# Gated DeltaNet mixer: triangular inverses kept at 64x64 blocks, the rest solved on v with two heads on the partitions

## The chip, the cores and the metric

The kernel runs on one core of a Trainium2 chip. The metric is the device time of one execution in microseconds. Its engines are PE (TensorE, matrix products), DVE (VectorE), ACT (ScalarE), POOL (GpSimd) and SP (SyncE); the last two issue most of the DMAs here. They run side by side, each through its own list of instructions in order, and wait for one another on semaphores.

## The reference, cut to what matters

The program is a trunk of two layers over 256 tokens of width 2048, in f32. Layer 0 mixes tokens with a gated delta rule, layer 1 with sparse attention; behind each mixer stand a convolutional gated feed-forward block and a gated embedding. Only layer 0's mixer changes:

```python
proj = x @ w_in                                  # q, k, v, z and the gates
qkv = silu(causal_dwconv(qkv, conv_w))
diff = gc[..., :, None] - gc[..., None, :]
decay = where(tri, exp(where(tri, diff, 0.0)), 0.0)
lmat = where(strict, einsum('bhncd,bhnsd->bhncs', kb, k) * decay, 0.0)
amat = lmat + eye(C)
sol = triangular_solve(amat, rhs, left_side=True, lower=True, unit_diagonal=True)
```

`amat` is unit lower triangular, one for each head and chunk; solving with it on the values gives u, from which the outputs follow. The kernel works the same recurrence with chunks of 128 tokens, so that there are two blocks, `a = 0, 1`, a head. There are 32 value heads of width 128.

## The kernel before

**Plan.** The order of all instructions is written by a planner, `Plan`. Each piece of work is a task, made by `add(engine, cost, emit, after, ...)`, with an estimated cost, tasks it follows (`after` in data, `behind` in order only), buffers that it takes and gives back (`take`, `give`, counted in `room`), a `rank` (lower first) and, for DMAs, a `tail` until the data has landed. `run` simulates the engines with these costs and emits each task when its engine is free and its inputs and buffers are. The order of each engine is thereby fixed when the program is built; the chip only adds the waits. The big weight products form one strict sequence on PE (ranks 4 and 5); the mixer's small products have rank 1 and are put between them as soon as the planner sees them ready.

**Weights.** Weights come as blocks of 128 x 1024 f32 through SP into `raw`; ACT or DVE rounds them to `hi` (L412, L416), DVE forms `lo = raw - hi` (L420), and PE multiplies in fp32r (L349, L352; L362, L363, L365). Products of plain f32 show as two records each.

**Mixer.** Heads go in 8 groups of four (`g`, `i` within a batch), groups in two batches of four. `decay_gates` computes the cumulated gates and stores them in DRAM as `grow` (L734); `decays` brings them back as rows, broadcast over the partitions (L829, on SP), into L and qd. `batch` makes L = `lmat` for each group (L989, L995; gram products L869), stores its 32x32 diagonal blocks (`lt`, L1006, on POOL) and its lower blocks (`lo`, L1013), loads all the diagonal blocks of a batch with one block on each partition (`ld`, L1019), inverts them by substitution in 31 steps on DVE (L1037, L1039), and stores the inverses plain and transposed (`tt`, L1042; `tu`, L1045).

`solve` builds from these the 128x128 inverse of each head and block `a`. On the partitions lie four heads with 32 rows each. `Lb`, `Gc` and `Tb` are loaded by 8 DMAs each (L899, L908, L905). For block distance d = 2, 1, 0 it computes `left` (L924: 1, 2 and 3 products for each `a`, of 32 to 96 columns), an eviction on ACT (L928), `right` (L933: one product for each `a`) and another eviction (L936). `Gc` then goes to DRAM as `gs` (L944), and `group` loads it into `pm` by 8 DMAs (`fill`, L1119), where each head's inverse lies as one 128x128 matrix.

`group` transposes v (`turn`, L1103), scales it (L1108) and for each block `a` multiplies by `pm` (`begin`, L1086, by way of the helper `mul`; four products of 128 columns) and evicts to u (`keep`, L1150). Between the two blocks stand `cross` (also L1086, with `n21`) and `cut` (L1138). `out` (L1164, L1165), the norm and the transposes that fill `oT` follow. The output products of group g (`mixes`) are placed between the weight blocks of group g + 2; those of the last two groups come after the mixer, and `project` takes oT of groups 6 and 7. The planner's order around the change depends on: 2 PSUM buffers `bk` and 2 `sp`, one `vt`, one `pm`, one `u`, four `L`. `conv` makes q, k and v (L559 to L573).

## Time and profile before

| what | us |
|---|---|
| median of 3 runs | 2768.59 (2767.57 to 2770.47) |
| the profiled execution's own time | 2768.83 |
| its span, first to last instruction | 2767.0 |
| PE busy | 2749.2 |
| DVE busy | 1871.4 |
| ACT busy | 1441.1 |
| POOL busy | 251.3 |

The engines overlap, so their busy times don't add up to the span. The granted PE clock is 0.998 of full speed over the span. A row of a timeline has the start and length in us, engine, line, operation, written tile and read tiles, shapes and count, and in brackets the idle time before it and what ended it. A row of groups has a count, busy us and mean ns, then the idle time before. Matmuls are pipelined: their recorded lengths overlap, and the distance from start to start is what one costs.

### The profile page before, as it was taken

Reading aid. Unit: us, or ns where it says so; the run is one execution under the profiler, and the core shown is the slowest. Engines: PE = TensorE matmul, PEld = TensorE weight load, DVE = VectorE, ACT = ScalarE, POOL = GpSimd, SP = SyncE. Lnnn points to the kernel's source line nnn. Section 1 sums busy time; section 2 is a strip of 40 time slices with the busy share of each in tenths; the row PEclk is TensorE's granted clock in tenths of the full one; section 3 lists DMA queues with packets and bytes.
Section 4 is the critical chain, followed back from the end, with each engine's and each line's share of the span. In section 5 each row is a group of like instructions: output and inputs, shape, how many; then the busy total and the mean of one; then the engine's idle time right before and its main releaser. Section 6 shows DMA issues by size and latency. Waiting matters only on the chain.

```text
span 2767.0 us, 39746 instructions
## 1 busy us (share of the span) xinstructions
PE 2749.2 (99%) x14796; PEld 2373.6 (86%) x14796; DVE 1871.4 (68%) x2964; ACT 1441.1 (52%) x2314; POOL 251.3 (9%) x437
## 2 busy tenths in 40 slices
PE   9999999999999999999999999999999999999999
PEld 8878888888888888888888888988888888888887
DVE  7887679866778666666546766775766666655575
ACT  6766565655555455555434444455555555543343
POOL 0324212034000000000000000300000000000000
PEclk9999999999999999999999999999999999999999
DMA  7776657666655766665557456545656666655655
GB/s 216 221 216 179 183 172 218 191 177 194 173 164 184 220 192 209 209 198 186 195 191 238 158 185 216 173 153 169 194 173 195 199 195 192 196 192 190 214 173 190
DMA packets 418434, 531.43 MB, mean 192 GB/s; under 512 B 24476, under 2 KB 305792, under 8 KB 418240
## 3 DMA queue, kind: packets, MB, share of 16 engines
q1 hardware_dynamic: 401424, 499.81, 57.7%
q0 software_dynamic: 16128, 28.49, 3.8%
q8 instruction: 116, 1.90, 0.3%
q14 instruction: 78, 0.64, 0.1%
q10 hardware_dynamic: 688, 0.59, 0.1%
HBM read 517.74 MB, written 14.20 MB: 192 GB/s over the span
## 4 chain that ended last, share of the span: by engine, by line
PE 96%; DMA 2%; DVE 1%; POOL 0%; ACT 0%; issue 0%; SPq 0%; ACTq 0%
PE mm_ps L352 33%; PE mm_ps L349 17%; PE b_ps L362 13%; PE b_ps L363 13%; PE b_ps L365 13%; DMA raw<-in_gdn_w_in 1%; PE s_ps L1086 1%; PE s_ps L924 1%; PE o_ps L1165 1%; DMA pm<-gs 0%; PE n_ps L1397 0%; PE lg_ps L1736 0%; PE sc_ps L1653 0%; PE s_ps L933 0%; DMA tu<-ld 0%; DMA gs<-Gc 0%
## 5 line engine op out<-in xcount | busy, mean ns | idle before, releaser
L420 DVE TENSOR_TENSOR lo<-raw,hi 128x1024 fp32r<-128x1024 f32 (+1 forms) x906 | 1103.6, 1219 | 707.7 <-ACT hi L412 695.1
L412 ACT ACTIVATE hi<-raw 128x1024 fp32r<-128x1024 f32 (+1 forms) x871 | 918.3, 1054 | 1085.7 <-PE mm_ps L352 504.3
L352 PE MATMUL mm_ps<-xT,hi 128*128 128x512 f32 (+1 forms) x4136 | 1012.4, 393 | 3.8 <-DVE pd L562 2.6
L352 PEld LDWEIGHTS mm_ps<-xT,hi 128*128 128x128 f32 (+1 forms) x4136 | 755.8, 188 | 151.5 <-issue 3.7
L349 PEld LDWEIGHTS mm_ps<-xT,lo 128*128 128x128 f32 (+1 forms) x4136 | 532.2, 191 | 20.2
L349 PE MATMUL mm_ps<-xT,lo 128*128 128x256 f32 (+1 forms) x4136 | 544.3, 284 | 0.0
L362 PE MATMUL b_ps<-hi,xT 128*128 128x512 f32 (+2 forms) x678 | 260.4, 385 | 2.9 <-ACT hi L412 2.9
L363 PE MATMUL b_ps<-hi,xT 128*128 128x512 f32 (+2 forms) x678 | 258.3, 382 | 0.0
L362 PE MATMUL b_ps<-hi,hTA 128*128 128x512 f32 x512 | 199.2, 389 | 0.0
L363 PE MATMUL b_ps<-hi,hTA 128*128 128x512 f32 x512 | 199.2, 389 | 0.0
L365 PE MATMUL b_ps<-lo,xT 128*128 128x512 f32 (+2 forms) x678 | 180.7, 383 | 0.0
L362 PEld LDWEIGHTS b_ps<-hi,xT 128*128 128x128 f32 x678 | 127.8, 188 | 26.4 <-ACT hi L412 3.1
L363 PEld LDWEIGHTS b_ps<-hi,xT 128*128 128x128 f32 x678 | 127.9, 189 | 23.3
L365 PEld LDWEIGHTS b_ps<-lo,xT 128*128 128x128 f32 x678 | 124.8, 189 | 22.8
L365 PE MATMUL b_ps<-lo,hTA 128*128 128x512 f32 x512 | 136.9, 389 | 0.0
L1436 POOL DMA_DIRECT2D lng<-in_ln_g x16 | 8.7, 546 | 1335.8 <-DVE x L1442 1333.2
L363 PEld LDWEIGHTS b_ps<-hi,hTA 128*128 128x128 f32 x512 | 96.1, 188 | 20.0
L362 PEld LDWEIGHTS b_ps<-hi,hTA 128*128 128x128 f32 x512 | 96.1, 188 | 20.0
L365 PEld LDWEIGHTS b_ps<-lo,hTA 128*128 128x128 f32 x512 | 96.1, 188 | 19.9
L362 PE MATMUL b_ps<-hi,oT 128*128 128x512 f32 (+1 forms) x258 | 102.9, 399 | 0.1
L363 PE MATMUL b_ps<-hi,oT 128*128 128x512 f32 (+1 forms) x258 | 100.4, 389 | 0.0
L569 DVE SCALAR_TENSOR_TENSOR ac<-pd,cw,ac 128x256 f32<-128x256 f32 x192 | 90.6, 482 | 4.3 <-ACT ac L566 0.7
(333 smaller groups left out, 2599.6 us busy)
## 6 DMA issues: line engine op xcount, KB each, us to landing
raw<-in_gdn_w_in SPq DMA_DIRECT2D x191, 512.0 KB, 4.1
raw<-in_ffn_w_down SPq DMA_DIRECT2D x160, 512.0 KB, 3.9
raw<-in_ffn_w_up SPq DMA_DIRECT2D x158, 512.0 KB, 3.8
raw<-in_ffn_w_gate SPq DMA_DIRECT2D x157, 512.0 KB, 4.2
raw<-in_dsa_w_in SPq DMA_DIRECT2D x72, 512.0 KB, 3.6
raw<-in_gdn_w_o SPq DMA_DIRECT2D x64, 512.0 KB, 3.9
raw<-in_ple_w_gate SPq DMA_DIRECT2D x56, 512.0 KB, 4.4
raw<-in_dsa_w_o SPq DMA_DIRECT2D x32, 512.0 KB, 4.3
```

Source lines behind the costliest of these rows:

```text
L349: nc.tensor.matmul(ps[o][:m, S:], lo[:, k, o * P:o * P + m], xk[:, 0], start=False, stop=e)
L352: nc.tensor.matmul(ps[o][:m], hi[:, k, o * P:o * P + m], xk.rearrange("p a b -> p (a b)"), start=s, stop=e)
L362: nc.tensor.matmul(ps[o][:, c], xh, hi[:, k, c], start=s, stop=False)
L363: nc.tensor.matmul(ps[o][:, c], xl, hi[:, k, c], start=False, stop=False)
L365: nc.tensor.matmul(ps[o][:, c], xh, lo[:, k, c], start=False, stop=e and c.stop == n)
L412: nc.scalar.activation(hi, box["raw"], AF.Copy)
L420: nc.vector.tensor_tensor(lo, box["raw"], box["hi"].bitcast(F32), op=ALU.subtract)
L569: nc.vector.scalar_tensor_tensor(box["ac"], pd[:, k:k + S], wt[:, k:k + 1], box["ac"], op0=ALU.mult, op1=ALU.add)
L924: nc.tensor.matmul(ps[:, a, 32 * (e - d - 1):], Lb[:, a, PAIR[e, d]], Gc[:, a, e, 32 * e:], start=e == d + 1, stop=e == 3)
L1086: nc.tensor.matmul(ps[:, h], lhs[:, h], rhs[:, h], start=True, stop=True)
L1165: nc.tensor.matmul(ps[:, h], qd()[:, a, h], u()[:, a, h], start=not a, stop=True)
L1436: d = add(G, 0.55, lambda r=r, src=src: nc.gpsimd.dma_start(out=r(), in_=bass.AP(tensor=src.tensor, offset=src.offset + nb * 512, ap=[[0, ...
```

## The change

Inverses are built only up to 64x64. `solve` now has one level: `left` and `right` make four products each of 32 columns, one for each (block `a`, half `n`), with four heads on the partitions; two evictions go to `Gy` and `Gx`. `Lb`, `Gc` and `Tb` are loaded by 4 DMAs each. There is no `gs`: `group` fills the diagonal 32x32 blocks of `pm` straight from `tt` by 8 DMAs, and the off-diagonal block from `Gx` by 4 (`place_`, from SBUF to SBUF). A matrix in `pm` now holds two heads, each with a 64x64 inverse on its part of the diagonal.

The step from 64 to 128 is done on v: the upper half is multiplied by its inverse (`begin`, n = 0), copied to `ua`, multiplied by the lower left 64x64 block of L (`lower`), taken from the lower half of v (`minus`), which then meets its own inverse (`begin`, n = 1). That block of L is transposed on DVE (`flip`), stored in DRAM (`spare`, 4 DMAs a group) and loaded into `LB` (`across`, 4 DMAs). The right sides hold two heads on the partitions, 64 tokens each: the Silu of v's conv writes block 0 in that order (two calls, not one), and block 1 is brought to it by `less`, eight calls on 64 partitions that replace the four of `cut` and write to `vp`. The results are evicted to u by calls on 64 partitions that write to other partitions than they read (`keep`).

Beside that: `grow` is stored by two DMAs so that a group's rows are one run; the layout of L and qd is by head and then block; the `lo` stores are 2 a group, not 3; the scale `svp` is copied in that layout; some `tail`s given to the planner are larger; `vp`, `ua`, `LT`, `LB` and `Gx` are single buffers. The core of the diff:

```diff
-        pm, Tb, Lb, Gc = new("pm", [8, P]), new("Tb", [2, 3, P]), new("Lb", [2, 6, P]), new("Gc", [2, 4, P])
-        PAIR = {(e, d): e * (e - 1) // 2 + d for e in range(1, 4) for d in range(e)}
+        pm, Tb, Lb, LB = new("pm", [2, 4, P]), new("Tb", [4, P]), new("Lb", [4, P]), new("LB", [2, 2, P])
+        Gc, Gy, Gx = (new(k, [4, 32]) for k in ("Gc", "Gy", "Gx"))
...
+                        nc.scalar.activation(tile()[:, 0].rearrange("p (n r t) -> p n r t", n=2, r=2)[:, :, c],
+                                             box["ac"][:, :P].rearrange("p (n t) -> p n t", n=2), AF.Silu)
+                        nc.scalar.activation(tile()[:, 1, c * P:c * P + P], box["ac"][:, P:], AF.Silu)
...
-                self.grow = self.dr.tile([64, P], F32, tag="grow", name="grow", bufs=1)
-                nc.gpsimd.dma_start(out=self.grow, in_=gr)
+                self.grow = self.dr.tile([32, 2, P], F32, tag="grow", name="grow", bufs=1)
+                for a in range(2):
+                    nc.gpsimd.dma_start(out=self.grow[:, a], in_=gr[32 * a:32 * a + 32])
...
         def rows_into(g, dm):
-            nc.sync.dma_start(out=dm, in_=bass.AP(tensor=self.grow.tensor, offset=self.grow.offset + 4 * g * P,
-                                                  ap=[[0, P], [32 * P, 2], [1, 4 * P]]))
+            nc.sync.dma_start(out=dm.rearrange("p h a t -> p (h a t)"),
+                              in_=bass.AP(tensor=self.grow.tensor, offset=self.grow.offset + 8 * g * P,
+                                          ap=[[0, P], [1, 8 * P]]))
...
         def solve(s, i):
 
...
+            def spread(tile, name, first):
+                def put(h):
+                    hs = slice(32 * h, 32 * h + 32)
+                    src = s[name][i, h].rearrange("a b p c -> p (a b) c")[:, first::2]
+                    nc.gpsimd.dma_start(out=tile[hs, :, hs] if tile is not Gc else tile[hs], in_=src)
+                return put
...
+            tt, tu = [], []
+            for tile, name, key, first, got, rank in ((Gc, "tt", "t", 1, tt, R["fetch"]), (Tb, "tu", "u", 0, tu, R["fetch"])):
+                put = spread(tile, name, first)
+                for h in h4:
+                    got.append(add(G, 0.55, lambda h=h, put=put: put(h), [s[key]], behind=got[-1:],
+                                   take=["Gc" if tile is Gc else "Tb"] * (not h), tail=5.0, rank=rank))
+            s["lb", i] = []
+            for n in h4:
+                s["lb", i].append(add(G, 0.55, lambda n=n: across(n), s["LT", i],
+                                      behind=s["lb", i][-1:] or s.get(("lb", i - 1), chained["lb"])[-1:],
+                                      take=["LB"] * (not n), tail=4.0, rank=R["keep"]))
+            chained["lb"] = s["lb", i]
...
+            def left():
+                ps = box["ps"] = sps("bk", [4, 32], "s_ps")
+                for n in h4:
+                    nc.tensor.matmul(ps[:, n], Lb[:, n], Gc[:, n], start=True, stop=True)
+
+            def right():
+                ps = box["ps"] = sps("bk", [4, 32], "s_ps")
+                for n in h4:
+                    nc.tensor.matmul(ps[:, n], Tb[:, n], Gy[:, n], start=True, stop=True)
+            y = add(E, 0.9, left, [*lo, *tt], take=["bk", "Gx"], give=["Lb", "Gc"], rank=1)
+            y = add(A, 0.3, lambda: nc.scalar.activation(Gy, box["ps"], AF.Copy), [y], give=["bk"], rank=1)
+            y = add(E, 0.9, right, [y, *tu], take=["bk"], give=["Tb"], rank=1)
+            s["x", i] = add(A, 0.3, lambda: nc.scalar.activation(Gx, box["ps"], AF.Identity, scale=-1.0), [y],
+                            give=["bk"], rank=1)
+
+        chained = dict(lb=[], pm=[])
...
+                        nc.gpsimd.dma_start(out=s["lt"][i, :, :, c].rearrange("h a i j -> i (h a) j"),
+                                            in_=ha(L[g]()[32 * c:32 * c + 32, :, :, 32 * c:32 * c + 32]))
+                    stored.append(add(G, 0.6, store, [p], tail=3.5))
+                LT = lazy(lambda: new("LT", [8, 64]))
+
+                def flip(g=g, LT=LT):
+                    nc.vector.transpose(LT()[64:], ha(L[g]()[64:, :, :, :64]))
+                f = add(V, 0.6, flip, [p], take=["LT"], rank=3)
+                s["LT", i] = []
+                for n in range(4):
+                    def spare(n=n, i=i, LT=LT):
+                        e, d = n // 2, n % 2
+                        nc.gpsimd.dma_start(
+                            out=s["lb"][i, :, :, 32 * d:32 * d + 32, 32 * e:32 * e + 32].rearrange("h a p c -> p (h a) c"),
+                            in_=LT()[64 + 32 * e:96 + 32 * e, :, 32 * d:32 * d + 32])
+                    s["LT", i].append(add(G, 0.6, spare, [f], give=["LT"] * (n == 3), behind=s["LT", i][-1:], tail=4.0,
+                                          rank=R["keep"]))
...
-                    def keep(e=e, g=g, i=i):
+                for n in range(2):
+                    def keep(n=n, g=g, i=i):
                         nc.gpsimd.dma_start(
-                            out=s["lo"][i, :, :, PAIR[e, 0]:PAIR[e, 0] + e].rearrange("q i d j -> i q (d j)"),
-                            in_=L[g]()[32 * e:32 * e + 32, :, :, :32 * e].rearrange("p a h j -> p (a h) j"))
-                    s[i].append(add(G, 0.6, keep, [p], give=["L"] * (e == 3), tail=3.0, rank=R["keep"]))
...
                 def turn(j=j, box=box):
                     ps = box["ps"] = sps("sp", [2, 2, P], "v_ps")
-                    for a in range(2):
-                        for r in range(2):
-                            nc.tensor.transpose(ps[:, a, r], VT[g][j]()[:, r, a * P:(a + 1) * P], self.ident)
+                    for n in range(2):
+                        nc.tensor.transpose(ps[:, 0, n], VT[g][j]()[:, 0, n * P:n * P + P], self.ident)
+                    for r in range(2):
...
-                for a in range(2):
-                    def fill(a=a, d=d):
-                        nc.gpsimd.dma_start(out=pm[32 * d:32 * d + 32, 4 * a:4 * a + 4, 32 * d:],
-                                            in_=s["g", i][:, :, a, d, 32 * d:].rearrange("h j c -> j h c"))
-                    ld.append(add(G, 0.55, fill, [s["st", i]], behind=ld[-1:], take=["pm"] * (not ld), tail=3.0, rank=R["fill"]))
+            for h in h4:
+                j, r = h // 2, h % 2
+                for e in range(2):
+                    def fill(h=h, j=j, o=64 * r + 32 * e, e=e):
+                        nc.gpsimd.dma_start(out=pm[o:o + 32, j, :, o:o + 32],
+                                            in_=s["tt"][i, h].rearrange("a b p c -> p (a b) c")[:, e::2])
+                    ld.append(add(G, 0.55, fill, [s["t"]] if ld else [s["t"], s["x", i]], behind=ld[-1:] or chained["pm"], take=["pm"] * (not ld), tail=5.0,
+                                  rank=R["fill"]))
+            for h in h4:
+                def place_(h=h, j=h // 2, o=64 * (h % 2)):
+                    nc.gpsimd.dma_start(out=pm[o:o + 32, j, :, o + 32:o + 64], in_=Gx[32 * h:32 * h + 32])
+                ld.append(add(G, 0.55, place_, [s["x", i]], behind=ld[-1:], give=["Gx"] * (h == 3), tail=4.0, rank=R["fill"]))
+            chained["pm"] = ld[-1:]
 
             qd, qo, n21, wq, fd, wd = fr[g]
             v_ = R["last"] if last else 2
             u, ud = lazy(lambda: new("u", [2, 4, P])), []
+            vp = lazy(lambda: new("vp", [4, P]))
...
+                    def less(n, j, box=box):
+                        ns = slice(64 * n, 64 * n + 64)
+                        for r in range(2):
+                            h = 2 * j + r
+                            nc.vector.scalar_tensor_tensor(
+                                vp()[64 * r:64 * r + 64, 2 * j + n], box["ps"][ns, h], s["nc1"][ns, 4 * i + h:4 * i + h + 1],
+                                vt()[ns, 1, h], op0=ALU.mult, op1=ALU.add)
+                    x = add(E, 0.95, cross, [*d, fd[1]], take=["bk"], give=["n21"], rank=1)
+                    d = []
+                    for n in range(2):
+                        for j in range(2):
+                            x = add(V, 0.5, lambda n=n, j=j, less=less: less(n, j), [x, *td], take=["vp"] * (not n and not j),
+                                    give=["bk", "L" if last else "vt"] if n and j else [], rank=v_)
+                        d.append([x])
+                else:
+                    d = [d, d]
+                last_of = []
...
+                    box = {}
+
+                    def begin(a=a, n=n, y=y, box=box):
+                        ps = box["ps"] = sps("bk", [2, P], "s_ps")
+                        for j in range(2):
+                            nc.tensor.matmul(ps[:, j], pm[:, j, 2 * a + n], y()[:, 2 * j + n], start=True, stop=True)
+
+                    def keep(r, a=a, n=n, box=box):
+                        return (u()[64 * n:64 * n + 64, a].rearrange("p (j r) c -> p r j c", r=2)[:, r],
+                                box["ps"][64 * r:64 * r + 64])
+                    x = add(E, 0.45, begin, [*d[n], *(ld if not n and not a else [])], take=["bk"],
+                            give=["pm", "vp"] if a and n else [], rank=1)
+                    if not n:
+                        ua = lazy(lambda: new("ua", [2, P]))
+                        z = add(A, 0.41, lambda ua=ua, box=box: nc.scalar.activation(ua(), box["ps"], AF.Copy), [x],
+                                take=["ua"], rank=0.8)
+                        more = {}
+
+                        def lower(a=a, ua=ua, more=more):
+                            ps = more["ps"] = sps("sp", [2, P], "s_ps")
+                            for j in range(2):
+                                nc.tensor.matmul(ps[:, j], LB[:, j, a], ua()[:, j], start=True, stop=True)
+
+                        def minus(y=y, more=more):
+                            t = y().rearrange("p (j n) c -> p n j c", n=2)[:, 1]
+                            nc.vector.tensor_tensor(t, t, more["ps"], op=ALU.subtract)
+                        z = add(E, 0.45, lower, [z, *s["lb", i]], take=["sp"], give=["ua"] + ["LB"] * a, rank=1)
+                        z = add(V, 0.42, minus, [z, *d[1]], give=["sp"], rank=min(v_, 1.5))
+                        d[1] = [z]
+                    for r in range(2):
+                        last_of.append(add(A, 0.41, lambda r=r, keep=keep: nc.scalar.activation(*keep(r), AF.Copy), [x],
+                                           take=["u"] * (not a and not n and not r), give=["bk"] * r,
+                                           behind=last_of[-1:] + ([z] if not n else []) if 0 else last_of[-1:], rank=1))
+                d = last_of
+                ud.append(last_of)
```

More of the change, by code (lines that the diff above doesn't have):

```diff
@@ L264, in build @@
         nc.gpsimd.memset(Lb, 0.0)
[L265 removed]
+        nc.gpsimd.memset(LB, 0.0)
         box1 = {}
@@ L747, in decay_gates @@
             y = add(V, 0.8, six, [y], give=["sp"], rank=1)
-            rows["go"] = add(G, 0.6, store, [y, b], tail=2.0)
+            rows["go"] = add(G, 1.2, store, [y, b], tail=2.0)
         rows = {}
@@ L892, in solve @@
         def solve(s, i):
-            wait, back = [], []
-            for q in range(8):
-                a, hs = q // 4, slice(32 * (q % 4), 32 * (q % 4) + 32)
-                def left(q=q, a=a, hs=hs):
-                    nc.gpsimd.dma_start(out=Lb[hs, a, :, hs], in_=s["lo"][i, q])
-                back.append(add(G, 0.55, left, s[i] if not q else [], behind=back[-1:], take=["Lb"] * (not q), tail=3.0, rank=R["keep"]))
-            def fetch(q, what):
-                a, hs = q // 4, slice(32 * (q % 4), 32 * (q % 4) + 32)
-                if what:
-                    nc.gpsimd.dma_start(out=Tb[hs, a, :, hs], in_=s["tu"][i, q, :3].rearrange("b n c -> n b c"))
-                    return
-                base = Gc[hs, a]
-                nc.gpsimd.dma_start(out=bass.AP(tensor=base.tensor, offset=base.offset,
-                                                ap=[list(base.ap[0]), [P + 32, 4], [1, 32]]),
-                                    in_=s["tt"][i, q].rearrange("b c n -> c b n"))
@@ L911, in solve @@
-            for what in range(2):
-                for q in range(8):
-                    back.append(add(G, 0.55, lambda q=q, what=what: fetch(q, what), [s["u"] if what else s["t"]],
-                                    behind=back[-1:], take=["Tb" if what else "Gc"] * (not q), tail=3.0, rank=R["fetch"]))
-            y = back
-            for d in (2, 1, 0):
-                n = 32 * (3 - d)
-                box = {}
-                def left(d=d, n=n, box=box):
-                    ps = box["ps"] = sps("bk", [2, n], "s_ps")
-                    for a in range(2):
-                        for e in range(d + 1, 4):
-                            nc.tensor.matmul(ps[:, a, 32 * (e - d - 1):], Lb[:, a, PAIR[e, d]], Gc[:, a, e, 32 * e:],
-                                             start=e == d + 1, stop=e == 3)
-                def keep(n=n, box=box):
-                    nc.scalar.activation(Gc[:, :, 3, :n], box["ps"], AF.Copy)
-                def right(d=d, n=n, box=box):
-                    ps = box["ps"] = sps("bk", [2, n], "s_ps")
-                    for a in range(2):
-                        nc.tensor.matmul(ps[:, a], Tb[:, a, d], Gc[:, a, 3, :n], start=True, stop=True)
-                def less(d=d, box=box):
-                    nc.scalar.activation(Gc[:, :, d, 32 * (d + 1):], box["ps"], AF.Identity, scale=-1.0)
-                y = add(E, 0.41 * (3 - d) + 0.05, left, y if d == 2 else [y], take=["bk"], give=["Lb"] * (not d), rank=1)
-                y = add(A, 0.2 + 0.0018 * n, keep, [y], give=["bk"], rank=1)
-                y = add(E, 0.46, right, [y], take=["bk"], give=["Tb"] * (not d), rank=1)
-                y = add(A, 0.2 + 0.0018 * n, less, [y], give=["bk"], rank=1)
@@ new lines, in across @@
+            def across(n):
+                j, r = n // 2, n % 2
+                rs = slice(64 * r, 64 * r + 64)
+                nc.gpsimd.dma_start(out=LB[rs, j, :, rs], in_=s["lb"][i, n].rearrange("a p c -> p a c"))
+            lo = []
+            for h in h4:
+                lo.append(add(G, 0.55, lambda h=h: nc.gpsimd.dma_start(
+                    out=Lb[32 * h:32 * h + 32, :, 32 * h:32 * h + 32],
+                    in_=s["lo"][i, h].rearrange("a b p c -> p (a b) c")),
+                    s[i], behind=lo[-1:], take=["Lb"] * (not h), tail=4.0, rank=R["keep"]))
@@ L1009, in batch @@
-                    stored.append(add(G, 0.6, store, [p], tail=2.5))
+                        nc.gpsimd.dma_start(out=s["lt"][i, :, :, c].rearrange("h a i j -> i (h a) j"),
[4 more added lines that the diff above has]
+                    nc.vector.transpose(LT()[64:], ha(L[g]()[64:, :, :, :64]))
@@ L1171, in sq @@
                                              accum_out=ss()[:, a, h // 2, h % 2:h % 2 + 1])
-                x = add(E, 1.85 if a else 0.95, out, [ud[a if last else 1], *fd], take=["bk"], give=["u", "qo", "qd"] if a else [], rank=1)
+                x = add(E, 1.85 if a else 0.95, out, [*ud[a if last else 1], *fd], take=["bk"], give=["u", "qo", "qd"] if a else [], rank=1)
                 for hs in ((0, 1), (2, 3)):
```

105 lines of the change are left out of this document (46 added, 59 removed).

## The prediction

> **What bounds the kernel now.** I read the page's engine totals and the chain of waits first, then busy time by stretch, then PE's waits.
>
> ```profile
> span 2767.0 us, 39746 instructions
> ...
> PE 2749.2 (99%) x14796; PEld 2373.6 (86%) x14796; DVE 1871.4 (68%) x2964; ACT 1441.1 (52%) x2314; POOL 251.3 (9%) x437
> ...
> PE 96%; DMA 2%; DVE 1%; POOL 0%; ACT 0%; issue 0%; SPq 0%; ACTq 0%
> ```
>
> PE (TensorE) is busy for all but 17.8 us, and 96% of the chain that ended last is PE's own work. So a change counts in two ways only: by PE time taken out or put in, and by moments at which PE stands still. The change touches the first mixer, which fills about the first 820 us. Each row below gives the stretch, its length, and busy us (instructions) of PE, then (second fence) of PE, PE's weight loads, DVE, ACT and POOL.
>
> ```profile
> 0.00:300.00 300.00, 287.92 (x1624) 0.99 0.70 204
> 300.00:800.00 500.00, 499.66 (x2789) 1.00 0.64 186
> ```
> ```profile
> 100.00:200.00 100.00, 94.44 (x491) 80.77 (x490) 85.50 (x167) 61.23 (x112) 26.76 (x48) 0.98 0.73 218
> ...
> 400.00:500.00 100.00, 99.84 (x533) 85.89 (x532) 88.79 (x174) 58.78 (x120) 22.52 (x39) 1.00 0.67 196
> ```
>
> From 300 to 800 us PE is never idle (0.3 us); whatever is saved there on PE is saved in the end. In the first 300 us it stands still for 12.1 us, for these reasons among others (total, times, longest):
>
> ```profile
> PE b_ps L362 <- ACT hi L412: 2.9, 1, 2.9
> PE mm_ps L352 <- DVE pd L562: 2.6, 1, 2.6
> PE s_ps L1086 <- DMA pm<-gs: 1.5, 2, 0.8
> ...
> PE s_ps L933 <- DMA Tb<-tu: 1.2, 1, 1.2
> PE s_ps L924 <- DMA Tb<-tu: 1.1, 1, 1.1
> ```
>
> The last three, 3.8 us, belong to the inverses that the change rewrites.
>
> **PE work.** A matmul of plain f32 shows as two records. Per group of four heads, the code before makes 12 products in `left` (L924) and 6 in `right` (L933). The records bear it out: 192 = 8 groups x 12 x 2, 96 = 8 x 6 x 2.
>
> ```profile
> L924 PE MATMUL s_ps<-Gc,Lb x192: 190/275/329, 186.6 to 692.1; 128*128 128x32 f32 x96, 128*128 128x64 f32 x64, 128*128 128x96 f32 x32
> ```
> ```profile
> L933 PE MATMUL s_ps<-Gc,Tb x96: 190/275/276, 190.1 to 694.5; 128*128 128x32 f32 x32, 128*128 128x64 f32 x32, 128*128 128x96 f32 x32
> ```
>
> After it, `left` and `right` make 4 each, of 32 columns. The two products with `pm` stay at 4 each but are cut into halves of 2, and `lower` is new: 2 products of 128 columns for each of the two token blocks. So 18 + 8 = 26 products become 8 + 8 + 4 = 20, six fewer. The blocks in which they are sent stay at eight (six and two before; two, four and two after). What is one worth? The recorded 275 ns overlap, so I take start to start of whole blocks, from PE's timeline:
>
> ```profile
> 642.97 0.53 PE L924 MATMUL s_ps<-Gc,Lb 128*128 128x32 f32 x4
> 643.33 0.48 PE L362 MATMUL b_ps<-hi,xT 128*128 128x512 f32 x1
> ...
> 652.59 1.42 PE L924 MATMUL s_ps<-Gc,Lb 128*128 128x96 f32 x12
> 653.84 0.63 PE L1103 MATMUL v_ps<-ident,v 128*128 128x128 f32 x4
> ...
> 657.54 1.05 PE L1086 MATMUL s_ps<-vt,pm 128*128 128x128 f32 x8
> 658.35 2.10 PE L352 MATMUL mm_ps<-xT,hi 128*128 128x512 f32 x8
> ```
>
> Two products take 0.36 us, four 0.81, six 1.25: (1.25 - 0.36) / 4 = 0.2225 us for each further product, and a block's fixed part is the same before and after. The three have mostly 32, 128 and 32 to 96 columns and lie on one line, so the columns do not show. Six fewer are 1.34 us a group, **10.7 us** in eight groups. Bounds: 0.18 us a product (0.36 / 2) gives 8.6; nothing in the rows gives more than 0.2225. I take 10.7, as block counts are equal.
>
> The Trainium skill, TensorE: Matmul & The Clock Gate, section Back-to-back issue gap, speaks against this: there a warm matmul costs its columns / 2.4 GHz + 2.5 ns, by which the narrow products taken out would be nearly free and the 128-wide ones put in would not, and the net gain an estimated 1.9 us. The same page's section on LDWEIGHTS gives columns of the weights / 1.2 ns, some 107 ns a record whatever the moving width, an estimate of 0.21 us a product, and with that the rows agree.
>
> **Waits of the solve.** Of the 3.8 us, the 1.5 on `pm<-gs` lose their cause: the trip of `Gc` to DRAM and back (`gs`) is gone, `pm`'s diagonal comes straight from `tt`. The 2.3 on `Tb<-tu` stay possible: `right` still waits for `Tb`, though for 4 loads, not 8. Bounds 0 to 3.8 saved; I take the middle, 1.9, since the chain as a whole gets shorter:
>
> ```profile
> 167.33 0.55 POOL L1042 DMA_DIRECT2D tt<-xi  x1 [45.92 <-DVE wq L822]
> 171.31 0.54 POOL L1045 DMA_DIRECT2D tu<-ld  x1 [3.43 <-ACT ld L1044]
> ```
> ```profile
> L1086 PE MATMUL s_ps<-vt,pm x112: 270/275/377, 218.5 to 741.7; 128*128 128x128 f32 x112
> ```
> ```profile
> lt<-L POOLq DMA_DIRECT2D x32, 32.0 KB, 4.0
> ...
> tu<-ld POOLq DMA_DIRECT2D x2, 512.0 KB, 7.3
> Gc<-tt POOLq DMA_DIRECT2D x64, 16.0 KB, 4.2
> Tb<-tu POOLq DMA_DIRECT2D x64, 12.0 KB, 3.3
> ```
> ```profile
> L1006 POOL DMA_DIRECT2D lt<-L x32 | 18.6, 587 | 1.3 <-DMA lt<-L 0.9 <-DMA lo<-L 0.4
> ```
>
> Before, 51 us pass from `tt` (167.3) to the first product with `pm` (218.5). After: `tu` has landed at 171.3 + 7.3 = 178.6, four `Tb` loads at 0.59 and 3.3 to land make 184.3, `right` and its eviction some 3, then 12 fills of 0.59 and about 4.2 to land: 199, 19 us sooner. Against that, POOL's queue grows ahead of `ld<-lt`: 16 stores of the flipped block more and four `lo` stores fewer in the batch, 12 x 0.587 = 7 us that the first substitution, and all behind it, may come later. Twelve us of the lead remain, so this costs PE nothing; without the lead it would be the 7. All of POOL's issues count alike: 40 a group before, 38 after (4 lt, 4 lb, 2 lo, 4 Lb, 4 Gc, 4 Tb, 4 LB, 8 + 4 into pm). `LB` and `Gx` are single buffers, so POOL will stand behind `lower` and behind the fill of `pm` as it now stands behind L924; only later groups' loads and fills wait there.
>
> `grow` is stored in two issues, 0.59 us later; SP's row loads wait for it with weight loads behind them, and the 2.9 us on `hi` above sits at their end. On the other side each row is now one run of 4 KB, not two of 2 KB, which may free SP earlier. Bounds -2.9 to +0.6; I take 0, as I can't tell which is larger.
>
> **DVE, ACT.**
>
> ```profile
> L562 DVE TENSOR_TENSOR pd<-mm_ps,fold 128x256 f32<-128x256 f32 x64 | 24.3, 418 | 2.2 <-ACT fold L559 1.8
> ...
> L1138 DVE SCALAR_TENSOR_TENSOR vt<-s_ps,nc,vt 128x128 f32<-128x128 f32 x28 | 8.0, 344 | 8.2 <-PE s_ps L1086 8.2
> L810 DVE STREAM_TRANSPOSE xt<-sq 128x256 f32<-128x256 f32 x16 | 7.1, 441 | 1.0 <-ACT sq L804 0.7
> ```
> ```profile
> L559 ACT ACTIVATE fold<-mm_ps 128x256 f32<-128x256 f32 x64 | 20.9, 375 | 9.2 <-PE mm_ps L352 9.1
> ...
> L1150 ACT ACTIVATE u<-s_ps 128x512 f32<-128x512 f32 x16 | 9.6, 599 | 20.5 <-PE s_ps L1086 20.5
> ```
>
> DVE gets, per group, the flip of 512 elements (0.44 to 0.88 us by L810; I take the upper), eight `less` of 64 partitions for four `cut` (0 to 4 x 0.344 more; upper, as the free size stays) and two `minus` (2 x 0.418): 3.1 us, 25 us over the mixer. ACT gets ten evictions of 256 elements for two of 512 (3.75 against 1.2, 20 us in all); it loses four small ones a group and gets one more Silu call for each of 32 value columns, which I take as even; it is idle for 39 of 100 us. From 300 us on this lies beside PE's work: DVE's worst stretch, 400 to 500, has 11 us free, and the planner ranks its long job there, the second substitution (`solve1`, 5), behind the casts, so it gives way. From 100 to 200 it is different: DVE is 85% busy, and the 2.6 us of L352 are PE waiting for DVE. There the four flips add 3.5 us. Bounds 0 (they fit the 14.5 idle us) and 3.5; I take 2.0.
>
> **The last group** has little behind it. Its oT is complete on DVE and first used in the second half of the projection's first column block:
>
> ```profile
> 820.39 0.74 DVE L1211 SCALAR_TENSOR_TENSOR oT<-ot_ps,ng,oT 128x512 fp32r<-128x512 f32 x1
> ...
> 830.72 1.28 DVE L227 TENSOR_TENSOR x<-x,b_ps 128x512 f32<-128x512 f32 x2
> ```
> ```profile
> 850.39 0.39 PE L362 MATMUL b_ps<-hi,oT 128*128 128x512 f32 x1
> ...
> 853.11 0.39 PE L362 MATMUL b_ps<-hi,oT 128*128 128x512 f32 x1
> ```
>
> A block of two rows of weights takes 2.7 us on PE, so the half that ends before 830.7 began near 825; oT was there at 821.1, 4 us ahead. The new order adds `ua`, `lower` and `minus` between cross product and last u: 0.375 + 0.45 + 0.418 and the hand-overs, 2 to 4 us. Cover and delay are about equal; I take 0, and up to 2 for the range.
>
> **Sum.** The profiled execution took 2768.8 us (span 2767.0 and 1.8 around it), 0.2 from the median 2768.6 of the runs. 2768.8 - 10.7 - 1.9 + 2.0 = **2758.2 us**.
>
> **Rivals.**
> (a) More than that: all 3.8 us go, the `hi` wait goes (2.9), the flips fit: 2768.8 - 10.7 - 6.7 = 2751.4. For it: the shorter chain. Against: these waits come from DMA and DVE, which stay busy. 0.12.
> (b) The gain is eaten at the start: the 7 us of POOL's queue come through to PE, with the 2.0 of the flips: 2768.8 - 10.7 + 9.0 = 2767.1. For it: `ld` waits for every store. Against: the 12 us of lead. 0.12.
> (c) Columns set the price of a product: at 0.2225 for 128 columns, 1024 columns taken out a group are 1.78 us and 768 put in 1.34, so 3.6 us in all: 2765.2. Against it is the flat line above. 0.05. It is the rule of Back-to-back issue gap in the Trainium skill's TensorE page.
> (d) Slower: DVE becomes the bound through the mixer, so that PE waits for `lo` halves and conv sums for each us added: 2768.8 - 10.7 + 25 = 2783. It decides once DVE has no free time where it is asked, and breaks even at 10.7 of the 25. For it: 85 and 89% busy in two stretches. Against: 0.3 us of PE idle in 500. 0.06.
>
> **How the numbers follow.** The forecast has 0.65; its own range is 2754 (all 3.8 saved, flips free) to 2764 (nothing saved, 3.5 lost, 2 at the last group). About 0.2%, 5.5 us, is what a measurement here tells from no change, so faster means below 2763.1. The forecast with nearly all of its weight and (a) lie there: 0.77; (b), (c) and its tail are within: 0.17; (d) is slower. The range, 2751 to 2766, takes in (c) and most of (a) and leaves (b)'s upper half and (d) out.
>
> **What would show it.** PE should have 96 records fewer (14700) and some 10 us less busy time; L924's successor only blocks of eight; PE idle under 1 us from 300 to 800; the first product with `pm` near 200 to 210 us. Wrong it would be if PE's idle time grew by over 5 us, with DVE or a `pm`, `Tb` or `LB` load as releaser; or if PE's busy time fell by less than 6.

## The result and the profile after

The changed kernel takes 2752.5 us (median of 6 runs, 2750.3 to 2758.7), the kernel before 2768.1 (6 runs, 2764.8 to 2770.5): a ratio of 0.9946, 95% interval 0.9936 to 0.9957, or 15.5 us. The forecast was 2758.2. In the profiled executions the difference is 17.1 us (2768.8 and 2751.7). Medians here and below leave out one execution of the kernel with the wide products doubled, which took 4392.4 us at a granted clock of 0.653.

The page's totals for the changed kernel:

```profile
span 2749.9 us, 39712 instructions
...
PE 2736.2 (100%) x14700; PEld 2360.5 (86%) x14700; DVE 1893.3 (69%) x3023; ACT 1460.5 (53%) x2383; POOL 241.5 (9%) x422
```

PE is still the bound: 96 records and 13.0 us of busy time fewer, and 13.7 us idle instead of 17.8. Next, busy time by stretch in the changed kernel, with the columns of the prediction's fence (PE, PE's weight loads, DVE, ACT, POOL; granted clock; DMA):

```profile
0.00:300.00 300.00, 293.58 (x1651) 253.17 (x1652) 243.93 (x484) 203.87 (x416) 83.83 (x152) 0.99 0.70 206
300.00:800.00 500.00, 499.68 (x2763) 433.20 (x2762) 395.95 (x731) 307.00 (x625) 98.87 (x179) 1.00 0.61 179
100.00:200.00 100.00, 98.16 (x518) 83.32 (x517) 90.44 (x174) 67.35 (x127) 44.49 (x79) 1.00 0.79 230
400.00:500.00 100.00, 100.00 (x533) 85.78 (x532) 93.15 (x168) 62.09 (x129) 28.22 (x49) 1.00 0.67 203
```

From 300 to 800 us PE is idle for 0.3 us, as before, though DVE's worst stretch rose from 88.8 to 93.2 busy. From 100 to 200 us, where the prediction saw a loss, PE gained 3.7 us and the clock rose from 0.98 to 1.00. The reasons for which PE stands still, in the changed kernel (total, times, longest):

```profile
PE b_ps L362 <- DVE hi L416: 2.2, 1, 2.2
PE b_ps L362 <- ACT hi L412: 1.6, 1, 1.6
...
PE mm_ps L352 <- ACT zs L632: 0.9, 1, 0.9
PE s_ps L935 <- DMA Gc<-tt: 0.6, 1, 0.6
...
PE b_ps L362 <- DVE pd L562: 0.2, 1, 0.2
```

No wait on `pm` or `Tb` is left, and the 2.6 and 0.8 us behind `pd` and `v` have become 0.2 and 0.9.

A second thing shows only in the clock. PE's busy time by slices of 5 us, last but two the granted clock, first of before, then of the changed kernel:

```profile
75.00:80.00 5.00, 2.70 (x7) 2.19 (x8) 2.38 (x5) 3.81 (x9) 0.00 (x0) 0.77 0.38 120
80.00:85.00 5.00, 5.00 (x21) 4.02 (x21) 4.32 (x5) 4.98 (x14) 0.00 (x0) 0.88 0.89 288
...
175.00:180.00 5.00, 4.72 (x21) 4.22 (x22) 4.07 (x9) 3.90 (x10) 1.24 (x3) 0.67 0.85 323
```
```profile
80.00:85.00 5.00, 5.00 (x17) 3.95 (x16) 3.53 (x5) 4.58 (x12) 0.00 (x0) 0.66 0.63 185
...
175.00:180.00 5.00, 5.00 (x33) 4.48 (x32) 4.86 (x9) 4.05 (x11) 3.81 (x8) 1.00 1.04 352
```

After some of its waits PE works for a few microseconds at a lower clock. Busy time x (1 - clock) is what a slice loses: 4.72 x 0.33 = 1.56 at 175 us before, 5.00 x 0.34 = 1.70 at 80 us after. Summed over the mixer's slices, before lost 2.8 us and the changed kernel 1.7. "Slow clock" below is this sum.

All of the gain is there by the end of the mixer: the first transposes of the next stage start at 863.5 us before and at 846.6 after, 16.9 us sooner.

### The profile page after: what moved, and what is told of

Same layout as the page of the kernel before. It is cut to its first block, busy times and chain, and to the rows that moved or that the text cites. A ratio compares the mean times of both kernels' runs of the same rounds, so it can differ in the third digit from the quotient of the medians.

```text
span 2749.9 us, 39712 instructions
## 1 busy us (share of the span) xinstructions
PE 2736.2 (100%) x14700; PEld 2360.5 (86%) x14700; DVE 1893.3 (69%) x3023; ACT 1460.5 (53%) x2383; POOL 241.5 (9%) x422
## 4 chain that ended last, share of the span: by engine, by line
PE 97%; DMA 1%; DVE 1%; issue 0%; POOL 0%; ACT 0%; SPq 0%; DVEq 0%; ACTq 0%
PE mm_ps L352 34%; PE mm_ps L349 18%; PE b_ps L362 13%; PE b_ps L363 13%; PE b_ps L365 13%; PE o_ps L1230 1%; PE s_ps L1190 1%; PE n_ps L1462 0%; PE sc_ps L1718 0%; PE lg_ps L1801 0%; PE s_ps L1206 0%; PE s_ps L1105 0%; PE ot_ps L1269 0%; PE o_ps L1229 0%; PE g_ps L1083 0%; DMA cr<-in_gdn_conv_w 0%
```

## The experiments

Two things need an explanation: whether the price of a product is right, and where the 5.7 us beyond the forecast come from. Theory A, formed from the two traces: the load of the first substitution goes out 4.2 us sooner, because less stands ahead of it on POOL, so the substitution starts sooner (its first step by 1.6 us) and the stretch in which DVE is full ends before PE runs out of work. Its rivals are the lead and the waits as the prediction has them, and its (b), (c) and (d).

Times are medians; unless another is named, they stand beside 2752.5 for the changed kernel and 2768.1 for before. The kernel before, run beside them, had 2768.2 to 2769.0.

**What a product costs** (two runs on the changed kernel).

```diff
 def left():                      # and right() alike
-    nc.tensor.matmul(ps[:, n], Lb[:, n], Gc[:, n], start=True, stop=True)
+    for _ in range(2):
+        nc.tensor.matmul(ps[:, n], Lb[:, n], Gc[:, n], start=True, stop=True)
```

> The changed kernel, with each product of left and right (L935, L940; 32 columns, plain f32) issued twice into the same place of PSUM, so 64 products more in the mixer; the output is the same. They go in the same eight-product blocks, which double. My price of 0.2225 us for each further product, whatever its columns: 64 x 0.2225 = 14.2 us more, 2752.5 + 14.2 = 2766.7, and PE busy up by 13 to 15 us with 128 records more. Rival (c), columns set the price: 64 x 0.2225 x 32/128 = 3.6 us more, 2756.1.

```diff
 def begin():
-    nc.tensor.matmul(ps[:, j], pm[:, j, 2 * a + n], y()[:, 2 * j + n], start=True, stop=True)
+    for _ in range(2):
+        nc.tensor.matmul(ps[:, j], pm[:, j, 2 * a + n], y()[:, 2 * j + n], start=True, stop=True)
```

> The changed kernel, with each product of begin (L1190; 128 columns, plain f32) issued twice, so 64 more, the same number as in the run with narrow products doubled; the output is the same. Both prices are the same for 128 columns: 64 x 0.2225 = 14.2 us more, 2766.7. It is the measure beside the narrow run: by my price the two come out alike, by rival (c) this one is 10.6 us slower than the narrow one.

In both, the cost that the planner is given for the block is doubled too. Measured: narrow 2771.7 (+19.2), wide 2767.5 (+15.0). The planner also moves other work, so the price is read from PE's timeline. Narrow blocks with what follows them, in the changed kernel and with the products doubled:

```profile
226.75 0.98 PE L935 MATMUL s_ps<-Gc,Lb 128*128 128x32 f32 x8
227.56 0.64 PE L1269 MATMUL ot_ps<-ident,zs 128*128 128x128 f32 x4
```
```profile
234.62 1.86 PE L936 MATMUL s_ps<-Gc,Lb 128*128 128x32 f32 x16
236.32 1.07 PE L1271 MATMUL ot_ps<-ident,zs 128*128 128x128 f32 x8
```

Four products of 32 columns take 0.81 us, eight take 1.70: 0.89 / 4 = 0.2225 each. Wide blocks, in the changed kernel and doubled:

```profile
344.24 0.60 PE L1190 MATMUL s_ps<-vt,pm 128*128 128x128 f32 x4
344.60 1.20 PE L349 MATMUL mm_ps<-xT,lo 128*128 128x256 f32 x8
```
```profile
349.10 1.05 PE L1191 MATMUL s_ps<-vt,pm 128*128 128x128 f32 x8
349.91 1.20 PE L349 MATMUL mm_ps<-xT,lo 128*128 128x256 f32 x8
```

Two products of 128 columns take 0.36, four 0.81: 0.225 each. Each doubled product brings its own weight load (14828 in either run, 128 more). From 32 to 128 columns the price does not depend on them, and rival (c) falls: it would have had 0.056 for a narrow one. The totals agree once the clock is taken in. 14.2 us of products plus the change of slow clock (8.0 and 0.0 against 1.7) make +20.5 and +12.5 of PE busy; measured are +20.2 and +12.2. The profiled executions of the two are 9.3 us apart, and 8.0 of that is slow clock: the narrow run comes out slower because of its clock and, for the rest, its waits, not its products.

**POOL's order ahead of the first substitution** (changed kernel).

```diff
-    stored.append(add(G, 0.6, store, [p], tail=3.5))          # lt, four a group
...
-    s[i].append(add(G, 0.6, keep, [p], behind=[f, *stored[-4:]] * n, give=["L"] * n, ...))
+    s[i].append(add(G, 0.6, keep, [p], behind=[f], ...))
+    stored.append(add(G, 0.6, store, [p], behind=[*s["LT", i], *s[i][1:]], give=["L"] * (c == 3), tail=3.5))
```

> The changed kernel, with the order of stores that the prediction had in mind: in each group the four lt stores stand behind the four lb stores and both lo stores on POOL's queue, so the load ld, and with it the first substitution, comes some 20 x 0.58 = 12 us later at most and about 7 us later if the stores find free moments; nothing is added or left out. Prediction's step: the lead of the shorter chain covers it, 0 to 2 us more, 2752.5 to 2754.5. Theory A (the five us beyond the forecast came because the substitution, with the DVE stage that it fills, started 4 us earlier): PE waits for DVE between 160 and 190 us again, 3 to 5 us and 1.5 us of slower matmuls behind them, so 4 to 7 us more, 2757 to 2760. Rival (b) of the prediction: 7 to 9 us more, 2760 to 2762, with waits on pm or Tb.

Measured: 2777.8, 25.3 more than the changed kernel. The dose was larger than meant: each group's `lt` stores now wait for the flip of the one `LT` buffer. POOL's rows of the changed kernel and of this run, then PE's in this run:

```profile
115.45 0.57 POOL L1038 DMA_DIRECT2D ld<-lt  x1 [4.47 <-DMA lt<-L]
...
163.25 0.58 POOL L1061 DMA_DIRECT2D tt<-xi  x1 [32.41 <-issue]
```
```profile
152.98 0.57 POOL L1038 DMA_DIRECT2D ld<-lt  x1 [4.62 <-DMA lt<-L]
...
195.94 0.55 POOL L1061 DMA_DIRECT2D tt<-xi  x1 [41.21 <-issue]
```
```profile
199.69 0.76 PE L352 MATMUL mm_ps<-xT,hi 128*128 128x512 f32 x1 [10.01 <-DVE pd L562]
201.58 3.32 PE L352 MATMUL mm_ps<-xT,hi 128*128 128x512 f32 x7 [1.13 <-DVE pd L562]
```

`ld` came 37.5 us later. The price was not paid at `pm` but on DVE's `pd`, at the end of the substitution, and by the clock (10.2 us of slow clock, 8.5 more). So an `ld` this late costs through the stretch in which DVE is held, which the lead of the chain behind `tt` does not cover. As the dose differs from the expected one, its number tests neither side's figure, and what a delay of 7 us costs is not shown.

**An earlier load in the kernel before.**

```diff
-    back.append(add(G, 0.55, left, s[i] if not q else [], behind=back[-1:], ...))
+    back.append(add(G, 0.55, left, [*s[i], s["ld"]] if not q else [], behind=back[-1:], ...))
```

> The kernel before, with one thing moved: the eight Lb loads that stand between the lt stores on POOL's queue wait for the load ld, so ld can be issued up to 8 x 0.58 = 4.6 us earlier (115 instead of 119.7 us); its work is otherwise that of before. Theory A: the waits of 0.78 and 2.56 us on DVE near 172 to 178 us and the slower matmuls behind them (1.6 us) go, though the inverses keep their old form: 2768.1 - 4.9 = 2763 us, PE idle down by 3 us. Rival (the stall went because of the changed solve or the planner's other order, not by the earlier start): 2768 us within 1, with the waits still there.

Measured: 2772.3, 4.0 slower than before. `ld` was issued at 115.5 and the first step ran at 126.5, as early as in the changed kernel (before: 128.1). But the planner put 15 `lo` casts and 2 `pd` between the steps, and the substitution ended when it had ended before (166.5 against 166.8). The waits on `v` and `pd` stayed, at 1.3 and 2.6. An earlier start alone thus does not take them away, and theory A falls in this form. Why the median is 4 us higher is open: the profiled execution was its fastest (2767.8).

**How long the substitution holds DVE.** Both traces suggest a theory A': not the start of the substitution counts, but what the planner puts between its 31 steps. Before has 14 `lo` casts and 2 `pd` there, the changed kernel 12 and 1. First and last step, in before and in the changed kernel:

```profile
128.10 0.19 DVE L1037 TENSOR_TENSOR xt<-L,xi 128x31 f32<-128x31 f32 x1
...
166.55 0.22 DVE L1039 TENSOR_TENSOR xi<-xi,xt 128x31 f32<-128x31 f32 x1
```
```profile
126.53 0.19 DVE L1056 TENSOR_TENSOR xt<-L,xi 128x31 f32<-128x31 f32 x1
...
162.48 0.22 DVE L1058 TENSOR_TENSOR xi<-xi,xt 128x31 f32<-128x31 f32 x1
```

One run gives the kernel before that order, another lengthens the stretch in the changed kernel:

```diff
-            'solve0': 1.8,        # kernel before
+            'solve0': 0.5,
```

> The kernel before, with one number of the planner changed: the rank of the first substitution's steps (solve0) 0.5 instead of 1.8, so that on DVE 12 lo casts and no pd stand between its first and its last step, where before has 14 and 2 (the changed kernel has 12 and 1); nothing else is edited. Theory A' (the wait near 175 us and the slow matmuls behind it come from how long the substitution holds DVE, whatever form the inverses have): the substitution ends some 3.3 us earlier, the waits of 0.78 and 2.56 us go and 1.6 us of slow clock with them: 2768.1 - 4.9 = 2763 us. Rival (the wait goes because of the changed solve itself, or PE only waits for lo instead): 2768 us within 1.5.

```diff
 def step(...):                    # changed kernel, first batch
+    for _ in range(2 if not b and 10 <= i <= 20 else 1):
         nc.vector.tensor_tensor(tv, ..., op=ALU.mult)
```

> The changed kernel, with the product of each of eleven middle steps (i = 10 to 20) of the first substitution computed twice into the same tile: 11 x about 0.42 us = 4.6 us more DVE work in exactly that stretch, no instruction of any engine in another place, the output the same. Theory A' (PE runs out of free PSUM just as the substitution ends, 0.16 us of waiting at 166.5 us says that no slack is left): 4.4 us of waiting come back, with up to 1.6 us of slow clock: 2757 to 2758.5. Rival (the stretch has slack again in the changed kernel, as the prediction's middle value for the flips assumed in part): at most 2 us, 2752.5 to 2754.5.

Measured: 2758.6 for the lengthened stretch (+6.1), as theory A' expects. PE's waits in it:

```profile
PE mm_ps L352 <- ACT zs L632: 3.0, 1, 3.0
PE b_ps L362 <- DVE pd L562: 2.3, 1, 2.3
...
PE mm_ps L349 <- DVE lo L420: 0.8, 1, 0.8
```

From 150 to 200 us these three were 0.9, 0.2 and 0 in the changed kernel; the last step ended at 167.3, 4.6 us later, and slow clock rose by 1.2. There is no slack: what is added there is paid in full. The other half of the theory fell: the kernel before, with its substitution from 126.4 to 162.3, took 2771.9 (ratio 1.0016, 1.0006 to 1.0025). Its waits:

```profile
PE s_ps L924 <- DMA Tb<-tu: 2.4, 1, 2.4
PE mm_ps L352 <- DVE pd L562: 1.7, 1, 1.7
...
PE s_ps L933 <- DMA Tb<-tu: 0.6, 1, 0.6
```

The 3.4 us on `v` and `pd` went down to 1.7 (0.7 on `zs` came in, as in the changed kernel), but the waits on `Tb` rose from 2.3 to 3.0 (4.1 with one behind 300 us), and 7.5 us of slow clock (2.8 before) outweighed the rest; the lowest slices lie from 180 to 200 us, right behind the wait of 2.4. So lengthening the stretch costs, but shortening it is not enough alone. How much of the gain in it belongs to the new solve, and how much to the planner's other choices, is not settled.

**DVE's cover** (changed kernel).

```diff
-    nc.vector.transpose(LT()[64:], ...)              # flip; less and minus twice too, first into scratch xt
+    for _ in range(2):
+        nc.vector.transpose(LT()[64:], ...)
```

> The changed kernel, with the flip, the eight less of a group and its two minus each issued twice (the first result goes to a scratch tile or is written over): 8 x 0.71 + 64 x 0.35 + 16 x 0.42 = 35 us more work for DVE over the mixer, the output the same, and no change to PE's work. Prediction (DVE's extra work lies beside PE's except in the stretch from 100 to 200 us): 2 to 5 us more, 2754.5 to 2757.5, with PE idle still under 1 us from 300 to 800 us. Rival (d), DVE becomes the bound of the mixer: up to 35 us more, 2787, with waits on lo and pd between 300 and 800 us.

Measured: 2778.3, 25.8 more, for 28.0 us of DVE busy time that the page shows (1921.3 against 1893.3). PE's waits from 300 to 900 us:

```profile
PE s_ps L1192 <- DVE vp L1213: 11.8, 6, 2.5
PE s_ps L1192 <- DVE vp L1173: 2.2, 4, 0.6
```

DVE is not full there (79% from 300 to 800 us in both runs), and the waits are not on `lo`, as rival (d) has it, but on the very results that were lengthened: `minus` (L1213) and `less` (L1173) lie in the chain between two products, and the planner, which was not told of the longer work, had placed the second product where the result used to be ready. So free time on DVE does not by itself hide such work. That a plan which knew its duration would hide it is likely but not shown, as no run told it. The two waits are 14.0 us. Slow clock rose by 1.1 and a wait on `zs` by 1.3; the rest of the 25.8 is not accounted for (the profiled execution, the fastest of four, is 22.5 us over the changed kernel's).

**`grow` alone, in the kernel before.**

```diff
-    nc.gpsimd.dma_start(out=self.grow, in_=gr)
+    for a in range(2):
+        nc.gpsimd.dma_start(out=self.grow[:, a], in_=gr[32 * a:32 * a + 32])
...                                # rows_into: one run of 8 * P, not two of 4 * P
```

> The kernel before, with the storing and loading of grow alone taken from the change: two stores instead of one, and each group's rows as one run of 4 KB a partition instead of two of 2 KB. Prediction took 0 within -2.9 to +0.6: 2768.1 us. If the shorter trip frees SP's queue for the weights behind it, the 2.9 us wait on hi near 78 us shrinks to at most 2.2, as in the changed kernel: 2767.4 or down to 2765.2.

Measured: 2764.3, 3.9 faster (ratio 0.9991, 0.9982 to 0.9999: 0.3 to 5.0 us). The wait near 78 us:

```profile
PE b_ps L362 <- DVE hi L416: 1.4, 1, 1.4
```

It fell from 2.9 to 1.4, and the 1.2 us of slow clock behind it are gone. That is 2.7 us at this place; later waits on `pd` (4.5, against 3.4 on `v` and `pd`) took a part of it back, so that the profiled spans differ by 1.8 alone. Whether the step is worth more than its bound of 2.9 the interval leaves open.

**One dependency of the solve, in the kernel before.**

```diff
-    y = back
+    y = back[:16]                 # left: Lb and Gc only
...
-    y = add(E, 0.46, right, [y], ...)
+    y = add(E, 0.46, right, [y, *back[16:]], ...)
```

> The kernel before, with one dependency of the solve as the change has it: left waits for the loads of Lb and Gc alone, and right for those of Tb; before, the first left of a group waits for all 24 loads. The inverses keep their form. If this dependency is what made the Tb waits, the 1.1 us of L924 on Tb go and those of right stay or grow: 2768.1 - 1 = 2767 us. If the Tb waits come from the length of the chain alone (tu, eight loads of 0.55 us), right takes over the whole wait: 2768 us within 1. Neither brings the changed kernel's 3.2 us on this place without the shorter loads.

Measured: 2776.8 beside 2769.0 (ratio 1.0032, 1.002 to 1.0045). Neither side expected it. PE's first blocks:

```profile
182.08 0.38 PE L924 MATMUL s_ps<-Gc,Lb 128*128 128x32 f32 x2 [1.61 <-DMA Gc<-tt]
188.71 0.61 PE L924 MATMUL s_ps<-Gc,Lb 128*128 128x32 f32 x2 [6.25 <-DMA Gc<-tt]
```

Freed of `Tb`, `left` is put earlier into PE's order, ahead of its loads, and PE stands 8.8 us on `Gc` up to 300 us, with all that is queued behind. A dependency taken away was no gain where the plan took the loads to land sooner than they did. The changed kernel also has larger `tail`s for those loads and stores; what they do alone no run here shows.

**The lead of the chain** (two runs on the changed kernel).

```diff
-    y = add(E, 0.9, left, [*lo, *tt], ...)
+    y = add(E, 0.9, left, [*lo, *tt, *tu], ...)
```

> The changed kernel, with left waiting for Tb's four loads too, as before's did; nothing else edited, though the planner orders the work anew around it. In the changed kernel the first left runs at 177.1 us and Tb's loads land near 181 us, so the chain of the first group gets some 3 to 4 us longer. By the prediction's lead (the first product with pm 22 us sooner than before): 0 to 1 us more, 2752.5 to 2753.5. Rival (the solve's waits of before come back): 2 to 4 us more with slow clock behind them, 2754.5 to 2757.

```diff
+    s["gx", i] = self.dr.tile([P, 4, 32], F32, ...)
+    nc.gpsimd.dma_start(out=s["gx", i], in_=Gx)
...
-    nc.gpsimd.dma_start(out=pm[o:o + 32, j, :, o + 32:o + 64], in_=Gx[32 * h:32 * h + 32])
+    nc.gpsimd.dma_start(out=pm[o:o + 32, j, :, o + 32:o + 64], in_=s["gx", i][32 * h:32 * h + 32])
```

> The changed kernel, with Gx taken to DRAM and back on its way into pm, as the old kernel did with Gc: one POOL store of 0.6 us more a group and one more landing of about 4 us between right and the fill of pm; nothing is left out. By the prediction's lead the 4.6 us are covered: 2752.5 to 2753.5. Rival (pm waits have only moved out of sight and have no reserve): waits on pm return, 1.5 us or more in the first groups and slow clock behind them, 2754 to 2757.

Measured: 2754.3 (ratio 0.9949, 0.9937 to 0.9962) and 2752.9 (0.9943, 0.9931 to 0.9955): neither differs from the changed kernel. The first product with `pm` in the second run:

```profile
202.81 0.94 PE L1195 MATMUL s_ps<-vt,pm 128*128 128x128 f32 x4 [0.70 <-DMA pm<-gx]
```

It is at 196.2 in the changed kernel. 6.6 us of a longer chain cost 0.7 us of waiting and no time that can be measured. Behind `tt` the lead holds.

**Four small copies** (changed kernel). They write `svp`, and stand on DVE straight ahead of the `hi` cast that PE waits for near 79 us.

```diff
-    nc.vector.tensor_copy(svp[64 * r:64 * r + 64, n], sv[64 * n:64 * n + 64, 0, :, r])
+    nc.gpsimd.tensor_copy(svp[64 * r:64 * r + 64, n], sv[64 * n:64 * n + 64, 0, :, r])
```

> The changed kernel, with the four small copies of sv into svp (64x8, 0.18 us each on DVE, forgotten in the prediction) done by GpSimd; they stand on DVE straight ahead of the hi cast for which PE waits 2.24 us near 79 us. If they are on that path, the cast comes 0.7 us earlier, the wait falls to about 1.5 us, and the time to 2751.8, or to 2750 if the slow clock behind the wait (1.7 us) goes too. If the cast waits for its weights, nothing changes: 2752.5.

Measured: 2749.5 (2748.6 to 2750.5), ratio to before 0.9931 (0.9918 to 0.9945): the fastest here, 3.0 us below the changed kernel, whose runs reach from 2750.3. The two intervals overlap (0.9936 to 0.9957 there), so the size of the step is not settled. DVE's rows in the changed kernel, then PE's in this run:

```profile
77.84 0.70 DVE L980 COPY svp<-sv 64x8 f32<-64x8 f32 x4
78.57 0.70 DVE L416 CAST hi<-raw 128x1024 fp32r<-128x1024 f32 x1
```
```profile
78.16 0.50 PE L362 MATMUL b_ps<-hi,xT 128*128 128x512 f32 x1 [1.39 <-DVE hi L416]
```

The wait fell from 2.24 to 1.39, and no slice of the mixer has a lower clock: 0.85 and 1.7 us, close to the 3.0. The 0.85 belongs to the copies; the 1.7 need not, as the run in which `left` waits for `Tb` has the copies and the wait but no lower clock.

## Why the prediction came out as it did

The forecast of 2758.2 was 5.7 us too high. The result lies outside its own range (2754 to 2764) and nearer rival (a), 2751.4, which had 0.12. It lies inside the given range because that was drawn to take in most of (a). The products were foreseen. The other two terms cancelled in the forecast (-1.9 and +2.0) and both came out as gains; that the miss stayed within the given range is to that extent luck. Term by term, in the profiled executions:

| term | predicted | measured |
|---|---|---|
| six products a group fewer | -10.7 | 48 x 0.2225 = -10.7 |
| waits of the solve | -1.9 | 3.8 to 0.6: -3.2 |
| flips, 100 to 200 us | +2.0 | waits 3.4 to 1.1, slow clock 1.6 to 0: -3.9 |
| `grow`, wait on `hi` | 0 | 2.9 to 2.2, slow clock 1.2 to 1.7: -0.2 |
| last group | 0 | +1.6, of another kind |
| sum | -10.6 | -16.4 of -17.1 |

**PE work** was right in price, count and reason: 14700 records, and a further product costs 0.2225 to 0.225 us at 32 and at 128 columns. The formula by columns in the Trainium skill's TensorE: Matmul & The Clock Gate, section Back-to-back issue gap, is not borne out for these plain f32 products: 0.89 us for four more narrow ones. But that section gives it for an isolated matmul, and says that it under-counts a stream with weight loads at few columns, so the trace does not contradict the page as a whole, which the prediction set against its own price.

**Waits of the solve** were right in kind; the middle of 0 to 3.8 was mis-sized by 1.3. The 2.3 us on `Tb` went too, and 0.6 on `Gc` stayed.

**The flips** are the step that failed, by 5.9 us. It added up DVE's new work in a full stretch and looked at nothing else there. The lengthened substitution shows that work in that stretch is indeed paid in full. But none of the four flips falls between its steps (126.53 to 162.48): two come before, two after.

```profile
125.79 0.71 DVE L1018 STREAM_TRANSPOSE LT<-L 64x512 f32<-64x512 f32 x1
...
171.75 0.71 DVE L1018 STREAM_TRANSPOSE LT<-L 64x512 f32<-64x512 f32 x1
```

Two `lo` casts and one `pd` left the stretch, the substitution ended 4.1 us sooner, and the wait of 2.6 us went together with the slow clock behind it. That the earlier end took the wait away is shown from one side only, by lengthening it; what else the new order does there stays open. That a wait carries a clock loss had no term at all.

**POOL's queue** had the wrong sign: not 7 us later but 4.2 sooner (`ld` at 115.5, from 119.7). The count of 12 more issues was right, their place was not: the planner put the 16 `lb` stores behind the `lt` stores, and took `Lb` loads and `lo` stores out from ahead of them. "Twelve us of the lead remain, so this costs PE nothing" left out a path, as the run with late `lt` stores shows (37.5 us later, not 7): the lead covers `pm`, not DVE. The working behind `tt` was close: 199 us forecast for the first product with `pm` from `tt` at 167.3, 31.7 us; measured 196.2 from 163.3, 33.0, and two runs with a longer chain show the reserve.

**`grow`** at 0 was mis-sized: alone it is worth 0.3 to 5.0 us (3.9 by the medians). In the changed kernel the four `svp` copies, which the prediction forgot, took back 0.85 us of waiting, and 1.7 us of slow clock followed that wait.

**DVE and ACT** from 300 us on: right, 0.3 us of PE idle. The reason given, 11 us of free DVE time, is not enough of one: the doubled run had DVE no fuller (79% from 300 to 800 us) and lost 25.8.

**The last group:** PE does not wait for oT, as predicted; 1.6 us appeared on an ACT cast of the projection's weights at 828 us, within the 2 allowed.

Of the rivals, (b) falls with its cause, which did not occur, (c) with the price, and (d) with the idle time from 300 to 800 us. (a) was right that the flips fit and that nearly all waits of the solve go, wrong that the `hi` wait goes (0.7 of 2.9).

## What to carry to other kernels

Count small f32 products, not their columns (32 to 128 here). In a kernel whose order is written out ahead, ask of each added operation which result stands behind it on its engine and who waits for that: four copies of 0.17 us cost 0.85 us of waiting here, 20 us of evictions next to none. In a stretch where one engine is full, list everything that the new order has there, not only what the change adds; and charge each wait of PE with the slow clock that may follow it.

## What the runs showed of the hardware

The clock behind a wait was not expected. Slices of 5 us around the same wait of 2.24 and 2.25 us near 79 us, in the changed kernel and in the run in which `left` waits for `Tb`:

```profile
75.00:80.00 5.00, 2.76 (x21) 2.48 (x21) 4.25 (x19) 5.00 (x14) 0.00 (x0) 1.00 0.14 45
80.00:85.00 5.00, 5.00 (x17) 3.95 (x16) 3.53 (x5) 4.58 (x12) 0.00 (x0) 0.66 0.63 185
```
```profile
75.00:80.00 5.00, 2.75 (x22) 2.52 (x22) 4.10 (x19) 5.00 (x14) 0.00 (x0) 1.00 0.16 52
80.00:85.00 5.00, 5.00 (x27) 4.24 (x27) 3.44 (x4) 4.73 (x12) 0.00 (x0) 1.00 0.62 185
```

PE was equally busy and waited equally long; the first lost 1.70 us of clock, the second nothing. So the length of the wait alone does not decide it, and this wait costs 2.2 or 3.9. A shorter one can cost more: with the narrow products doubled, 3.1 us of clock were lost behind a wait of 1.59.

```profile
201.62 2.62 PE L936 MATMUL s_ps<-Gc,Lb 128*128 128x32 f32 x16 [1.59 <-DMA Gc<-tt]
```
```profile
200.00:205.00 5.00, 3.41 (x22) 3.38 (x21) 0.00 (x0) 2.97 (x7) 1.09 (x3) 0.77 0.53 151
205.00:210.00 5.00, 5.00 (x20) 4.23 (x18) 2.42 (x3) 2.14 (x5) 3.97 (x8) 0.54 0.15 30
```

In the kernel before with the shorter stretch it was 6.0 us from 180 to 200, behind waits of 2.42 and 0.64. The Trainium skill, TensorE: Matmul & The Clock Gate, Part 1, has a clock at half speed after an idle window of about 3.4 us, and windows that run freely, whatever the kernel does. An estimate from that page, half of 3.4 us, gives the 1.7 us measured, though not the 3.1 and 6.0, and free windows fit that the same wait is punished in one run and not in another. That waits of 1.59 and 2.2 us can be enough, shorter than the page's window, is what the traces add; why some cost more than one window is open.

How much of the run-to-run spread (2750.3 to 2758.7 for the changed kernel) comes from this, no run here shows.
